# A Hyena encoder layer with a SwiGLU mixer: the way into the gate products, the last gate/up pair and the closing rows rewritten

## The chip, the cores and the metric

The kernel runs on one core of one Trainium2 chip. A core has TensorE (PE, which multiplies 128x128 weights into moving tiles of up to 512 columns and adds up in PSUM), VectorE (DVE), ScalarE (ACT), GpSimd (POOL) and SyncE (SP), each with its own in-order queue, and 16 DMA engines that the queues feed. The metric is the device time of one execution in microseconds; less is better.

## What is computed

One layer on a sequence of 1024 tokens with 1024 channels, in float32:

```
h = rmsnorm(x, norm_mix)
z = short_conv(h @ w_in + b_in);  x0, x1, v = split(z)          # 3 x 1024 channels
s = v * x1
y = irfft(rfft(s, 2L) * rfft(g, 2L))[:L] + s * skip              # g: filter made by a small MLP
x = x + (y * x0) @ w_out + b_out
x = x + (silu(n @ w_gate) * (n @ w_up)) @ w_down,  n = rmsnorm(x, norm_ffn)   # 2816 hidden
return rmsnorm(x, norm_final)
```

## The kernel before

Every product is done in three matmuls on split numbers: each operand is a high part rounded to the matmul's format ("fp32r") and a low part, the rest; high x high, high x low and low x high are added up in PSUM. `split(hi, lo, src)` casts the high part on ScalarE (L129) and subtracts on VectorE (L130). `low_dma(hi, lo, src)` makes the low part another way: ScalarE writes minus the high part (L149) and a DMA from GpSimd's queue adds the source to it (L150).

**Mixer, up to L1045.** The order of every engine is the order of the code (`manual_schedule`). At its end the last channel block goes through the inverse transform (`inverse`, `inverse_mm`, `finish`, `gate`) while TensorE multiplies the earlier blocks by `w_out`: `out_part(m, ks)` adds channel blocks `ks` of output columns 0 to 511 for the token blocks m and m + 4. Then `x1_half` adds such a half to the residual on VectorE, and ScalarE squares it and sums the squares into `sq2`.

**Into the gate products, L1236 to L1300.** TensorE, VectorE and ScalarE follow the code here, too. For the eight token blocks in the order `seq`, TensorE makes the other 512 columns (`out_mm`, 24 matmuls), `x1_half` adds them, `normed` scales by the reciprocal root of the mean square, `turn` transposes on TensorE, and `top_left` (blocks 0 to 3) or `top_sums` (blocks 4 to 7) make the moving operands of the gate and up products from the transposes. These products use a two-by-two block scheme with seven products instead of eight: of the normalised input they need the blocks B11, B21 (in `u2` for tokens 0 to 511), B22, T4 (in `u2` for tokens 512 to 1023) and the sums T1, T2, T3. Of each, `...h` is the high and `...l` the low part; in `u2` these are `uh` and `ul`.

**Gate/up pairs, `pair(i)`, i from 0 to 10.** A `Unit` is one of the two matrices for 256 hidden columns. It has products named by their weights' letter: a (`p1`, B11), f (T2), g (T3), e (T1), b (`p2`, B21), d (T4), c (B22), 12 matmuls each. a and b share a PSUM bank `pa`, f has `pb` (both in tile `...ab`); e and c share `pd`, g and d share `pc` (both in tile `...dc`). VectorE adds the banks into `uu` (L1203 after f, L1207 after g) and into the outputs (L1213 after e, L1217 after d and c). A product waits for VectorE when it writes a tile of which a bank is still to be read. The weights' operands rotate through five slots (`OPS`). For pair 0, part of them is made ahead (`pre`, `pq`, `wg0f` and so on). In the pairs only SP follows the code; TensorE, VectorE and ScalarE follow the order of a list scheduler that simulates the program when it is built. The gated products go to DRAM (`HD`) through GpSimd's queue, those of pair 10 through SP's (`held`).

**Down, from L1353.** Seven products `p1` to `p7` of 132 matmuls each add up in four PSUM banks (`bx`, `by`, `bz`); operands come from DRAM into raw slots `hr` (`HRAW`) and `wd`, which take over slots of the pairs (the tiles of T1, T2, T3 and `u2` among them) once those are read. The last product holds back three batches so that the four banks end one after another: for each, `scale(j)` adds, squares, takes the root on ScalarE, corrects the reciprocal by a Newton step, scales the two halves of a row block and stores them.

Of the kernel before, what the change touches and what calls it, by code (L numbers as in the profile page):

```python
# [102 lines left out]
def hyena_ffn_kernel(ctx: ExitStack, tc: tile.TileContext, a: dict, out: bass.AP):  # L103
# [377 lines left out]
    F_, Z_ = {}, {}  # L481

    class Filter:
# [534 lines left out]
    wo_split(1, 3)  # L1018

# [12 lines left out]
    def x1_half(j, h, o):  # L1032
        c = slice(h * 512, (h + 1) * 512)
        V.tensor_tensor(x1[j][:, c], x1[j][:, c], o, ALU.add)
        S.activation(
            slot("junk", f"jq{j}{h}", (512,)), x1[j][:, c], AF.Square, accum_out=sq2[j][:, h : h + 1]
        )
        load(X1D[j][:, c], x1[j][:, c])

    for m in range(4):  # L1040
        out_part(m, (NB - 1,))
        for q, j in enumerate(PAIRS[m]):
            x1_half(j, 0, po[m][:, q * 512 : (q + 1) * 512])
            V.tensor_scalar(sq2[j][:, 0:1], sq2[j][:, 0:1], 1.0 / D, EPS, ALU.mult, ALU.add)
# [12 lines left out]
    def normed(j):  # L1057
        w = small(f"rq{j}", 32, tag="rs1", bufs=2)
        sc, rt, r0, q = (w[:, i : i + 1] for i in range(4))
        V.scalar_tensor_tensor(sc, sq2[j][:, 1:2], 1.0 / D, sq2[j][:, 0:1], ALU.mult, ALU.add)  # L1060
        S.sqrt(rt, sc)
# [4 lines left out]
        for h in range(2):  # L1066
            d = x1[j][:, h * 512 : (h + 1) * 512]
            V.scalar_tensor_tensor(d, d, r0, gffn[:, h * 512 : (h + 1) * 512], ALU.mult, ALU.mult)

# [17 lines left out]
    def top_sums(m, pt):  # L1087
        ms = cols_of(m)
        if m < 3:
            tt = slot("inv", f"tt{m}", (4, 4, P))  # L1090
            t3, t2, t1, t4 = (tt[:, i] for i in range(4))
        else:
            ta, tb = slot("s1", "tta", (2, 4, P)), slot("xz", "ttb", (2, 4, P))
            t3, t2, t1, t4 = ta[:, 0], ta[:, 1], tb[:, 0], tb[:, 1]
        left = x1[m].rearrange("p (i k m) -> p i k m", i=2, k=4)
        b12, b22 = pt[:, 0:4], pt[:, 4:8]

        def part(nm, src, eng):
            hi, lo = tops[nm]
            S.copy(hi[:, :, ms], src)  # L1100
            n = 4 // len(lo)
            for x, l in enumerate(lo):
                ks = slice(x * n, (x + 1) * n)
                eng.tensor_tensor(l[:, :, ms], src[:, ks], hi[:, ks, ms].bitcast(F32), ALU.subtract)
# [3 lines left out]
        V.tensor_tensor(t2, b22, t1, ALU.subtract)
# [18 lines left out]
    OPS = ("fwd2", "vz", "s1", "xz", "sT")  # L1127
# [9 lines left out]
    class Unit:  # L1137
        def __init__(u, i, w, nm):
            u.nm = f"{nm}{i}"
# [24 lines left out]
        def sum_tiles(u):  # L1164
            u.s = slot(u.s_tag, f"{u.nm}s", (4, 4, P))

        def product(u, pt, x, src, bn, first, t=None):
            t = w_op(f"{u.nm}{x}", src) if t is None else t
            b = b_op(bn)
            for k in range(4):  # L1170
# [28 lines left out]

        def middle(u, early=False):  # L1200
            t = u.early if early else {}
            u.product(u.pb, "f", u.s[:, 1], "T2", True, t.get("f"))
            V.tensor_tensor(u.uu[:, 1], u.uu[:, 0], u.pb, ALU.add)  # L1203
# [3 lines left out]
            V.tensor_tensor(u.uu[:, 2], u.uu[:, 1], u.pc, ALU.add)  # L1207
            u.product(u.pd, "e", u.s[:, 0], "T1", True, t.get("e"))

        def end(u, out, early=False):  # L1210
            if not early:
                u.sum4()
            V.tensor_tensor(out[:, 2], u.uu[:, 2], u.pd, ALU.add)  # L1213
            u.product(u.pc, "d", u.a22, "T4", False)
            u.product(u.pd, "c", u.s[:, 3], "B22", False)
            u2b = u.uu[:, 1:2].broadcast_to([P, 2, 512])
            V.tensor_tensor(out[:, 0:2], u2b, u.dc.rearrange("p (q c) -> p q c", q=2), ALU.add)  # L1217
# [18 lines left out]
    with tc.manual_schedule(  # L1236
# [3 lines left out]
        for n, j in enumerate(seq):  # L1240
# [32 lines left out]
        ug.begin()  # L1273
        uu_.begin(True)
        ug.sums(V)
# [267 lines left out]
```

## Time and profile before

| what | value |
|---|---|
| median of 3 runs | 1182.83 us (1182.07 to 1184.84) |
| profiled execution, its own time | 1182.12 us |
| span of that execution, first to last instruction | 1180.3 us |
| mean granted TensorE clock | 0.995 |
| busy: PE, DVE, ACT, POOL | 1154.2, 875.5, 516.7, 151.2 us |

A row of a timeline has start, duration, engine, line, operation, output and inputs, and in brackets the idle time before it with what ended it. A row of waits has the engine that waited, what it was about to do, what it waited for, and the sum, the count and the longest in us. A row of the chain has start, duration, engine, tile and line. Matmuls overlap: the record of one lasts 0.39 us, and the next starts 0.23 us after it.

### The profile page before, as it was taken

What the parts mean: (1) busy time and instruction counts of PE and PEld (TensorE: products, weight loads), DVE (VectorE), ACT (ScalarE), POOL (GpSimd) and SP (SyncE); (2) the same over time, 40 slices, a digit from 0 to 9 for tenths busy, and PEclk for the clock granted to TensorE, in tenths of its full rate; (3) what the DMA queues carried; (4) which work ended last, traced back from release to release, by engine and by line L of the source; (5) the groups of instructions that cost most, each with busy time, mean ns of one, the idle gap of its engine ahead of it and who ended that gap; (6) DMA issues with size and microseconds to landing.
All of it is one profiled execution on the core that took longest, in us unless ns stands there. A gap on an engine that the chain in (4) does not pass through costs nothing.

```text
span 1180.3 us, 15139 instructions
## 1 busy us (share of the span) xinstructions
PE 1154.2 (98%) x5714; PEld 969.9 (82%) x5714; DVE 875.5 (74%) x1414; ACT 516.7 (44%) x820; POOL 151.2 (13%) x216
## 2 busy tenths in 40 slices
PE   8999999999999999898999999999999989999997
PEld 6889898898988987786888888888888868888885
DVE  7688988989898894588747676566666468956675
ACT  7563553545445473465333322332333233334444
POOL 0010211112011140043101110011001100111000
PEclk9999999999999999999999999999999999999999
DMA  7556778686675899443313232223323369842323
GB/s 236 147 120 144 141 164 166 159 174 149 131 154 109 206 242 271 135 117 72 118 61 125 99 133 89 91 97 126 107 72 113 111 193 365 302 121 89 98 81 143
DMA packets 100568, 170.32 MB, mean 144 GB/s; under 512 B 7052, under 2 KB 60684, under 8 KB 100367
## 3 DMA queue, kind: packets, MB, share of 16 engines
q0 software_dynamic: 24832, 78.39, 28.7%
q1 hardware_dynamic: 75661, 90.96, 23.6%
q8 instruction: 45, 0.74, 0.3%
q14 instruction: 28, 0.23, 0.1%
q10 hardware_dynamic: 2, 0.00, 0.0%
HBM read 101.96 MB, written 40.11 MB: 120 GB/s over the span
## 4 chain that ended last, share of the span: by engine, by line
PE 49%; DVE 4%; DMA 3%; issue 2%; ACT 1%; SPq 0%; POOL 0%; POOLq 0%; ACTq 0%; DVEq 0%
PE bx L1416 7%; PE po L914 3%; PE bz L1416 3%; PE by L1416 3%; DVE wd L1459 1%; PE wg0dc L1172 1%; PE wu9dc L1172 1%; PE wu8dc L1172 1%; PE wu7dc L1172 1%; PE wg9dc L1172 1%; PE wg8dc L1172 1%; PE wg7dc L1172 1%; PE wu6dc L1172 1%; PE wg6dc L1172 1%; PE wu5dc L1172 1%
## 5 line engine op out<-in xcount | busy, mean ns | idle before, releaser
L140 PE MATMUL z<-uh,whl 128*128 128x512 f32 x704 | 195.5, 393 | 0.0
L140 PEld LDWEIGHTS z<-uh,whl 128*128 128x128 f32 x704 | 130.1, 188 | 25.5
L1416 PE MATMUL bx<-wop,hop 128*128 128x512 f32 x480 | 111.1, 391 | 1.3 <-ACT hop L129 0.8
L140 PE MATMUL z<-ul,whl 128*128 128x512 f32 x352 | 108.8, 390 | 0.0
L1416 PEld LDWEIGHTS bx<-wop,hop 128*128 128x128 f32 x480 | 89.8, 188 | 21.4 <-ACT hop L129 1.2
L130 DVE TENSOR_TENSOR hop<-hrp,hop 128x1024 fp32r<-128x1024 f32 (+1 forms) x40 | 45.1, 1128 | 49.4 <-ACT hop L129 49.4
L129 ACT CAST hop<-hrp 128x1024 fp32r<-128x1024 f32 (+1 forms) x40 | 39.0, 977 | 91.9 <-PE bx L1416 44.6
L140 PEld LDWEIGHTS z<-ul,whl 128*128 128x128 f32 x352 | 66.1, 188 | 14.0
L914 PE MATMUL po<-wohl,uh 128*128 128x512 f32 x256 | 74.7, 394 | 1.8 <-DVE sig L669 1.4
L1027 POOL DMA_DIRECT2D hd<-g x40 | 21.6, 543 | 323.9 <-DVE g L1332 188.1
L1416 PE MATMUL by<-wop,hop 128*128 128x512 f32 x264 | 60.2, 389 | 0.0
L1416 PEld LDWEIGHTS by<-wop,hop 128*128 128x128 f32 x264 | 49.6, 188 | 10.3
L914 PEld LDWEIGHTS po<-wohl,uh 128*128 128x128 f32 x256 | 47.3, 188 | 12.4 <-DVE sig L669 1.6
L194 ACT CAST whl<-wt 128x1024 fp32r<-128x1024 f32 x24 | 25.2, 1049 | 68.7 <-PE z L140 64.7
L129 ACT CAST wop<-wd 128x512 fp32r<-128x512 f32 x73 | 42.2, 617 | 17.8 <-PE by L1416 9.2
L541 PE MATMUL pg<-hw,fwd 128*128 128x128 f32 x256 | 49.6, 275 | 0.0
L540 PE MATMUL pg<-hw,fwd 128*128 128x128 f32 x256 | 49.5, 275 | 0.0
L130 DVE TENSOR_TENSOR wop<-wd,wop 128x512 fp32r<-128x512 f32 x73 | 47.6, 684 | 1.5 <-ACT wop L129 1.5
L150 POOL DMA_DIRECT2D whl<-wt x24 | 20.8, 866 | 217.7 <-ACT whl L149 130.6
L1027 POOL DMA_DIRECT2D hrp<-hd x42 | 22.3, 531 | 187.0 <-DVE hop L130 166.9
L914 PE MATMUL po<-wohl,ul 128*128 128x512 f32 x128 | 44.3, 390 | 0.0
L540 PEld LDWEIGHTS pg<-hw,fwd 128*128 128x128 f32 x256 | 39.5, 192 | 0.6
(1586 smaller groups left out, 2834.9 us busy)
## 6 DMA issues: line engine op xcount, KB each, us to landing
hrp<-hd POOLq DMA_DIRECT2D x35, 512.0 KB, 4.0
wt<-in_hy_w_in_dram SPq DMA_DIRECT2D x24, 512.0 KB, 5.0
whl<-wt POOLq DMA_DIRECT2D x24, 512.0 KB, 4.6
wgr<-in_ffn_w_gate_dram SPq DMA_DIRECT2D x22, 512.0 KB, 4.1
wur<-in_ffn_w_up_dram SPq DMA_DIRECT2D x22, 512.0 KB, 3.9
wd<-in_ffn_w_down_dram SPq DMA_DIRECT2D x44, 256.0 KB, 6.6
hd<-g POOLq DMA_DIRECT2D x40, 256.0 KB, 2.6
hd<-sx POOLq DMA_DIRECT2D x30, 256.0 KB, 3.0
```

The costliest lines, as they stand in the source:

```text
L129: S.copy(hi, src)
L130: (eng or V).tensor_tensor(lo, src, hi.bitcast(F32), ALU.subtract)
L140: T.matmul(pt[:, h * 512 : (h + 1) * 512], w[wi], u2[ui][h][:, k, :], start=first and ti == 0, stop=last and ti == len(TERMS) - 1,)
L150: G.dma_start(lo.bitcast(F32), src, accum_op=ALU.add)
L194: S.copy(whl[:, 0], w_raw[n])
L540: T.matmul(o, fwd[r][:, j, :], f.hw[:, j, 0, :], start=True, stop=False)
L541: T.matmul(o, fwd[2 * r][:, jj, :], f.hw[:, jj, 1, :], start=False, stop=True)
L914: T.matmul(o, u2[yi][th][:, k, m * P : (m + 1) * P], wos[h][k // 2][wi][:, k % 2, :], start=(k == 0 and ti == 0), stop=(k == NB - 1 and ti ...
L1027: G.dma_start(dst, src)
L1172: T.matmul(pt, t[:, wi, k, :], b(k)[ui], start=first and k == 0 and ti == 0, stop=k == 3 and ti == len(TERMS) - 1, skip_group_check=not first,
L1416: T.matmul(pt, ho[hi_][:, x, q * P : (q + 1) * P], wo_[wi][:, x, :], start=fresh and first and x == 0 and ti == 0, stop=last and x == n - ...
L1459: V.tensor_tensor(w[:, dst], w[:, x], w[:, y], ALU.subtract)
```

## The change

1. `inverse_mm` of the last block stands between the parts of `out_part(.., (6,))` instead of behind all of them: eight matmuls come after it. `wo_load(1, 3)` uses another slot and is issued earlier. An instruction that loads ScalarE's square-root table stands behind the mixer's last split.
2. The squares are scaled by 1/32 while they are squared, so that their sums are means; the `sq2` correction (L1044) and its counterpart in `right` (L1474) go, and EPS is added where the two halves are.
3. `top_sums` becomes a class `Right` whose steps can be called one by one. The low parts of `top_left` for blocks 0 to 2, and for blocks 6 and 7 those of T4, for block 6 those of T3 and T1, are made by `low_dma`; of blocks 6 and 7 no low part is left on GpSimd's own arithmetic.
4. Blocks 6 and 7 and pair 0 are written out in a new order: block 6 is transposed before a of the gate unit, the steps of `Right` stand between the products, six matmuls of the up unit's b move behind g, and e, d and c of the gate unit follow each other, before f and g of the up unit. More weight operands of pair 0 are made ahead.
5. Pair 10 is `last_pair`: gate and up products interleaved, with TensorE in the order of the code. `HRAW` names other slots, and the last two slots of `OPS` change places.
6. The held-back batches of the last product follow the code on TensorE, VectorE and ScalarE, with the banks in the order 0, 2, 1, 3. `scale` takes the reciprocal of `sc / root + root`, with `gfin` doubled once, in place of the Newton step: three small VectorE operations behind the root instead of four. ScalarE scales and stores the right half first; the very last of these stores is issued from ScalarE's queue.

The core of the diff:

```diff
     wo_load(1, 2, "wt")
+    wo_load(1, 3, "hs")
     wo_split(1, 1)
     x1_load(5)
-    wo_load(1, 3, "whl1")
-    for m in range(3):
-        out_part(m, (6,))
+    out_part(0, (6,))
+    out_part(1, (6,), (0, 1))
     inverse_mm(b)
+    out_part(1, (6,), (2,))
+    out_part(2, (6,))
     finish(b)
...
     wo_split(1, 3)
+    S.sqrt(warm, ones)
...
         S.activation(
-            slot("junk", f"jq{j}{h}", (512,)), x1[j][:, c], AF.Square, accum_out=sq2[j][:, h : h + 1]
+            slot("junk", f"jq{j}{h}", (512,)),
+            x1[j][:, c],
+            AF.Square,
+            scale=1.0 / 32.0,
+            accum_out=sq2[j][:, h : h + 1],
         )
...
             x1_half(j, 0, po[m][:, q * 512 : (q + 1) * 512])
-            V.tensor_scalar(sq2[j][:, 0:1], sq2[j][:, 0:1], 1.0 / D, EPS, ALU.mult, ALU.add)
...
         S.copy(u2[0][0][:, :, ms], pt)
-        S.copy(x1[m].rearrange("p (k m) -> p k m", k=NB), pt)
+        xt = x1[m].rearrange("p (k m) -> p k m", k=NB)
+        S.copy(xt, pt)
+        if m < 3:
+            low_dma(u2[0][0][:, :, ms], u2[1][0][:, :, ms], xt)
+            return lambda: None
...
+        def low(t, nm, eng):
             hi, lo = tops[nm]
...
+                if eng is None:
+                    low_dma(hi[:, ks, t.ms], l[:, :, t.ms], t.src(nm)[:, ks])
+                else:
+                    eng.tensor_tensor(
+                        l[:, :, t.ms], t.src(nm)[:, ks], hi[:, ks, t.ms].bitcast(F32), ALU.subtract
+                    )
...
-    OPS = ("fwd2", "vz", "s1", "xz", "sT")
+    OPS = ("fwd2", "vz", "s1", "sT", "xz")
...
-        ug.begin()
+                ug.s_tag = "ab_d"
+                ug.split_sum_tiles()
+                ug.sums(V)
+        ug.begin(True)
         uu_.begin(True)
-        ug.sums(V)
-        low_dma(pq[:, 0, 0], pq[:, 0, 1], ug.a12)
-        normed(7)
+        r6 = Right(2, turns[6])
+        r6.sums12()
+        norm_begin(7)
+        r6.sum3()
+        r6.high("T2")
+        r6.b22_high()
+        norm_end(7)
+        ug.p1(pre[:, 0])
+        r6.high("T3")
+        r6.low("T3", None)
         early_op(pq[:, 1], uu_.a12)
-        ug.p1(pre[:, 0])
-        turn(6)
+        r6.low("T2", V)
+        r6.b22_low()
         ug.p1_out()
-        ug.early = {"f": w_op("wg0f", ug.s[:, 1])}
+        ug.early = {"f": w_op("wg0f", ug.s[1])}
         uu_.p1(pre[:, 1])
-        post(6)
-        post_late()
         turn(7)
+        r6.sum4()
+        r6.high("T1")
+        r6.low("T1", None)
         uu_.p1_out()
+        r7 = Right(3, turns[7])
+        r7.sums12()
+        r7.sum3()
         ug.p2(pq[:, 0])
-        post(7)
-        uu_.p2(pq[:, 1])
+        uu_.p2(pq[:, 1], (0, 1))
+        r6.t4_high()
+        r6.t4_low(None)
+        r7.part("T2", V)
+        r7.part("T3", V)
         ug.sum3()
...
+        ug.product(ug.pb, "f", None, "T2", True, ug.early["f"])
+        V.tensor_tensor(ug.uu[:, 1], ug.uu[:, 0], ug.pb, ALU.add)
+        r7.t4_high()
+        r7.t4_low(None)
+        r7.b22_high()
+        r7.b22_low()
+        ug.product(ug.pc, "g", None, "T3", True, ug.early["g"])
+        uu_.p2(pq[:, 1], (2, 3))
+        V.tensor_tensor(ug.uu[:, 2], ug.uu[:, 1], ug.pc, ALU.add)
+        ug.product(ug.pd, "e", None, "T1", True, ug.early["e"])
...
+        ug.end_products(g0[:, 1:4])
...
+    def last_pair(i):
...
+        ug.p1()
+        ug.p1_out()
+        ug.sums(V)
+        uu.p1()
+        uu.p1_out()
+        ug.product(ug.pb, "f", ug.s[1], "T2", True)
+        V.tensor_tensor(ug.uu[:, 1], ug.uu[:, 0], ug.pb, ALU.add)
+        ug.sum3()
+        ug.product(ug.pc, "g", ug.s[2], "T3", True)
+        V.tensor_tensor(ug.uu[:, 2], ug.uu[:, 1], ug.pc, ALU.add)
+        ug.p2()
+        S.activation(g[:, 0], ug.pa, AF.Silu)
+        ug.product(ug.pd, "e", ug.s[0], "T1", True)
+        uu.sums(V)
+        uu.product(uu.pb, "f", uu.s[1], "T2", True)
+        V.tensor_tensor(uu.uu[:, 1], uu.uu[:, 0], uu.pb, ALU.add)
+        ug.end(g[:, 1:4])
+        S.activation(g[:, 1:4], g[:, 1:4], AF.Silu)
+        uu.sum3()
+        uu.product(uu.pc, "g", uu.s[2], "T3", True)
+        V.tensor_tensor(uu.uu[:, 2], uu.uu[:, 1], uu.pc, ALU.add)
+        uu.p2()
+        V.tensor_tensor(g[:, 0], g[:, 0], uu.pa, ALU.mult)
+        uu.product(uu.pd, "e", uu.s[0], "T1", True)
...
-    HRAW = ("hs", "wt", "sT", "fwd2")
+    HRAW = ("hs", "wt", "fwd2", "s1")
...
+            for q in (0, 2, 1, 3) if held else range(4):
+                for x, ((ho, wo_), n) in enumerate(rest):
+                    mms(banks[q], ho, wo_, q, n, fresh, False, x == len(rest) - 1)
+                done(q)
...
-        V.scalar_tensor_tensor(sc, e, 1.0 / D, sqs[:, j : j + 1], ALU.mult, ALU.add)
+        V.scalar_tensor_tensor(sc, e, EPS, sqs[:, j : j + 1], ALU.add, ALU.add)
         S.sqrt(rt, sc)
-        V.reciprocal(r0, rt)
-        V.scalar_tensor_tensor(q, sc, -0.5, r0, ALU.mult, ALU.mult)
-        V.tensor_tensor(q, q, r0, ALU.mult)
-        V.scalar_tensor_tensor(r0, q, 1.5, r0, ALU.add, ALU.mult)
+        V.reciprocal(q, rt)
+        V.scalar_tensor_tensor(q, sc, q, rt, ALU.mult, ALU.add)
+        V.reciprocal(r0, q)
         a, b = y1[j][:, 0:512], y1[j][:, 512:1024]
+        S.activation(b, b, AF.Copy, scale=r0)
         V.scalar_tensor_tensor(a, a, r0, gfin[:, 0:512], ALU.mult, ALU.mult)
+        (S if j == NB - 1 else nc.sync).dma_start(ov[:, j, 512:1024], b)
         load(ov[:, j, 0:512], a)
-        S.activation(b, b, AF.Copy, scale=r0)
-        load(ov[:, j, 512:1024], b)
```

Where the code moves instructions, three pieces of the engines' order show it. The first is VectorE at the first residual halves (`x` a residual block, `po` the product's bank, `sq` the sums of squares, `rq` the small tile of `normed`). Before:

```order
L1034 TENSOR_TENSOR x_3689<-x_3689,po_3780 128x512
L1034 TENSOR_TENSOR x_3693<-x_3693,po_3910 128x512
L1044 TENSOR_SCALAR sq_3842<-sq_3842 128x1
L1034 TENSOR_TENSOR x_3776<-x_3776,po_3780 128x512
L1044 TENSOR_SCALAR sq_3842<-sq_3842 128x1
L1060 SCALAR_TENSOR_TENSOR rq_3939<-sq_3842 128x1
```

And of the change:

```order
L1037 TENSOR_TENSOR x_3672<-x_3672,po_3488 128x512
L1037 TENSOR_TENSOR x_3763<-x_3763,po_3488 128x512
L1037 TENSOR_TENSOR x_3674<-x_3674,po_3765 128x512
L1037 TENSOR_TENSOR x_3761<-x_3761,po_3765 128x512
L1037 TENSOR_TENSOR x_3678<-x_3678,po_3888 128x512
L1065 SCALAR_TENSOR_TENSOR rq_3917<-sq_3828 128x1
```

All eight adds now follow each other, and the add of the first other half (`po_3888`, before `po_3910`) stands behind them all, straight before the first small operation of its norm.

The second is ScalarE between block 6 and block 7 in pair 0 (`tt` and `tta`, `ttb` the sums of block 6 and of block 7, `wg0u` and `wu0u` the copies of a's banks, `wg0f` the operand of f). Before:

```order
L1185 COPY wg0u<-wg0ab 128x512
L129 CAST wg0f<-wg0s 128x512
L1106 COPY tt_4385<-tp_4360 128x512
L1100 CAST T2h<-tt_4385 128x4x128
L1100 CAST T3h<-tt_4385 128x4x128
L1100 CAST T1h<-tt_4385 128x4x128
L129 CAST uh_62<-tt_4385 128x4x128
L1116 CAST uh_62<-tp_4360 128x4x128
L1185 COPY wu0u<-wu0ab 128x512
L1106 COPY tta<-tp_4402 128x512
L1100 CAST T2h<-tta 128x4x128
```

And of the change:

```order
L149 ACTIVATE T3l_3957<-T3h 128x2x128
L153 CAST pq<-wur_4166 128x512
L149 ACTIVATE pq<-pq 128x512
L1250 COPY wg0u<-wg0ab 128x512
L129 CAST wg0f<-wg0sa 128x512
L1127 CAST T1h<-tt_4327 128x4x128
L149 ACTIVATE T1l<-T1h 128x4x128
L1250 COPY wu0u<-wu0ab 128x512
L1116 COPY tta<-tp_4381 128x512
L1149 CAST uh_62<-tt_4327 128x4x128
L149 ACTIVATE ul_64<-uh_62 128x4x128
L1127 CAST T2h<-tta 128x4x128
```

The copy `wg0u`, for which the gate unit's b waits, now stands behind block 6's T2, T3 and `pq`, and the negative copies for the lows (L149) stand between it and block 7's `T2h`.

The third is VectorE in pair 10 (`wg10..`, `wu10..` are the two units' operands and sums, `hop` and `wop` operands of the down stage, `g` the gated output). Before:

```order
L1213 TENSOR_TENSOR g_6995<-wg10u,wg10dc 128x512
L130 TENSOR_TENSOR wu10f<-wu10s,wu10f 128x512
L130 TENSOR_TENSOR wu10e<-wu10s,wu10e 128x512
L130 TENSOR_TENSOR hop12ct_g<-hrp_7329,hop12x_7331 128x1024
L1217 TENSOR_TENSOR g_6995<-wg10u,wg10dc 128x1024
L130 TENSOR_TENSOR wu10b<-wur_7122,wu10b 128x512
L1203 TENSOR_TENSOR wu10u<-wu10u,wu10ab 128x512
L1207 TENSOR_TENSOR wu10u<-wu10u,wu10dc 128x512
L130 TENSOR_TENSOR hop_7297<-hrp_7295,hop_7297 128x1024
```

And of the change:

```order
L1275 TENSOR_TENSOR g_6984<-wg10u,wg10dc 128x512
L130 TENSOR_TENSOR wu10b<-wur_6991,wu10b 128x512
L1477 TENSOR_TENSOR wu10u<-wu10u,wu10ab 128x512
L130 TENSOR_TENSOR wu10e<-wu10s,wu10e 128x512
L130 TENSOR_TENSOR wop_7290<-wd_7240,wop_7290 128x512
L130 TENSOR_TENSOR wop_7290<-wd_7241,wop_7290 128x512
L130 TENSOR_TENSOR wu10d<-wur_6991,wu10d 128x512
L1281 TENSOR_TENSOR g_6984<-wg10u,wg10dc 128x1024
L130 TENSOR_TENSOR wu10c<-wu10s,wu10c 128x512
L1482 TENSOR_TENSOR wu10u<-wu10u,wu10dc 128x512
L1484 TENSOR_TENSOR g_6984<-g_6984,wu10ab 128x512
L130 TENSOR_TENSOR hop_7287<-hrp_7285,hop_7287 128x1024
```

The add of the up unit's f (L1477, before L1203) now stands ahead of the wide sum of the gate unit's d and c and of every `hop`, and the first splits of the down weights (`wop`) stand ahead of the add after g (L1482).

More of the change, by code (lines that the diff above doesn't have):

```diff
@@ L1055, in t_op, with norm_begin, norm_end @@
         tops[nm] = (hi, lo)
[L1057 to L1061, printed above, removed]
+    def norm_begin(j):
+        w = rqs[j] = small(f"rq{j}", 32, tag="rs1", bufs=2)
+        V.scalar_tensor_tensor(w[:, 0:1], sq2[j][:, 1:2], EPS, sq2[j][:, 0:1], ALU.add, ALU.add)
+        S.sqrt(w[:, 1:2], w[:, 0:1])
+    def norm_end(j):
+        sc, rt, r0, q = (rqs[j][:, i : i + 1] for i in range(4))
         V.reciprocal(r0, rt)
@@ L1164, in sum_tiles, with split_sum_tiles, product @@
         def sum_tiles(u):
-            u.s = slot(u.s_tag, f"{u.nm}s", (4, 4, P))
-        def product(u, pt, x, src, bn, first, t=None):
+            t = slot(u.s_tag, f"{u.nm}s", (4, 4, P))
+            u.s = [t[:, q] for q in range(4)]
+        def split_sum_tiles(u):
+            ta, tb = slot("fwq", f"{u.nm}sa", (2, 4, P)), slot(u.s_tag, f"{u.nm}sb", (2, 4, P))
+            u.s = [ta[:, 0], ta[:, 1], tb[:, 0], tb[:, 1]]
+        def product(u, pt, x, src, bn, first, t=None, ks=range(4)):
             t = w_op(f"{u.nm}{x}", src) if t is None else t
             b = b_op(bn)
-            for k in range(4):
+            for k in ks:
                 for ti, (wi, ui) in enumerate(TERMS):
@@ L1212, in end @@
                 u.sum4()
[L1213 to L1217, printed above, removed]
+            u.end_products(out)
+            u.end_sums(out)
     seq = (0, 4, 1, 5, 2, 3, 6, 7)
@@ L1296, in hyena_ffn_kernel @@
+        ug.early["d"] = w_op("wg0d", ug.a22)
         uu_.sum_tiles()
         uu_.sums(V)
+        uu_.early["f"] = w_op("wu0f", uu_.s[1])
+        ug.end_products(g0[:, 1:4])
         uu_.sum3()
+        uu_.early["g"] = w_op("wu0g", uu_.s[2])
+        S.activation(g0[:, 0], ug.pa, AF.Silu)
+        ug.end_sums(g0[:, 1:4])
         uu_.sum4()
-        uu_.early = {}
+        uu_.product(uu_.pb, "f", None, "T2", True, uu_.early["f"])
+        V.tensor_tensor(uu_.uu[:, 1], uu_.uu[:, 0], uu_.pb, ALU.add)
@@ L1302, in hyena_ffn_kernel @@
+        uu_.product(uu_.pc, "g", None, "T3", True, uu_.early["g"])
     held = []
     def pair(i, ug=None, uu_=None):
-        put = store if i < NP - 1 else lambda *x: held.append(x)
-        g = slot("inv", f"g{i}", (4, 512))
         early = ug is not None
+        g = g0 if early else slot("inv", f"g{i}", (4, 512))
         if not early:
@@ L1431, in product2 @@
         rest = [(operands(nm, hx, wsrc, i, n), n) for i, n in BATCH[late:]]
-        for q in range(4):
-            for x, ((ho, wo_), n) in enumerate(rest):
-                mms(banks[q], ho, wo_, q, n, fresh, False, x == len(rest) - 1)
-            done(q)
+        with ExitStack() as order:
+            if held:
+                order.enter_context(
+                    tc.manual_schedule(
+                        engines={
+                            mybir.EngineType.PE,
+                            mybir.EngineType.DVE,
+                            mybir.EngineType.Activation,
+                        }
+                    )
+                )
+            for q in (0, 2, 1, 3) if held else range(4):
+                for x, ((ho, wo_), n) in enumerate(rest):
+                    mms(banks[q], ho, wo_, q, n, fresh, False, x == len(rest) - 1)
+                done(q)
     def four(fn, nm):
@@ L1502, in hyena_ffn_kernel @@
     load(gfin, a["norm_final"].partition_broadcast(P))
+    V.tensor_scalar(gfin, gfin, 2.0, None, ALU.mult)
     for i in range(NP):
```

160 lines of the change are left out of this document (106 added, 54 removed).

## The prediction

> **What bounds the kernel now.** I read the page's busy times first, then a table of engine times by stage, then TensorE's own waits.
>
> ```profile
> span 1180.3 us, 15139 instructions
> PE 1154.2 (98%) x5714; PEld 969.9 (82%) x5714; DVE 875.5 (74%) x1414; ACT 516.7 (44%) x820; POOL 151.2 (13%) x216
> ```
>
> TensorE is busy for 1154.2 of 1180.3 us and the change removes no matrix product, so at most 26 us can come back, plus whatever runs at a lowered clock. VectorE is not the bound: its work counts only where TensorE waits for it. The stages (columns after the stretch: length; then PE, PEld, DVE, ACT, POOL busy; granted clock; DMA share; GB/s):
>
> ```profile
> 448.00:490.00 42.00, 36.73 (x179) 29.92 (x178) 16.64 (x37) 15.46 (x29) 2.58 (x3) 1.00 0.76 231
> 528.00:556.00 28.00, 24.20 (x103) 18.32 (x102) 23.71 (x39) 16.33 (x30) 9.70 (x8) 0.94 0.37 72
> 556.00:944.00 388.00, 388.00 (x1714) 321.49 (x1713) 250.11 (x364) 119.08 (x183) 39.48 (x73) 1.00 0.31 103
> 944.00:955.00 11.00, 8.45 (x31) 6.51 (x30) 8.51 (x12) 4.61 (x7) 0.53 (x1) 0.84 0.39 121
> 980.00:1028.00 48.00, 47.89 (x212) 39.40 (x211) 44.17 (x67) 18.42 (x28) 3.76 (x8) 1.00 0.98 367
> 1164.00:1181.00 17.00, 7.67 (x33) 5.70 (x31) 8.27 (x28) 6.27 (x16) 0.00 (x0) 0.86 0.33 124
> ```
>
> The long middle, 556 to 944, has no idle TensorE at all. The idle time lies in four short places, and the change touches all four: the end of the mixer with the first residual halves (5.3 us idle), the first gate/up pair (3.8, with the clock at 0.94), the last pair (2.6, clock 0.84) and the closing rows. The waits name what is late there:
>
> ```profile
> PE tp L1073 <- DVE x L1068: 3.3, 1, 3.3
> PE wu10ab L1172 <- DVE wu10u L1203: 2.5, 1, 2.5
> PE wg0dc L1172 <- ACT wg0g L129: 1.9, 1, 1.9
> PE po L914 <- DVE sig L669: 1.4, 1, 1.4
> PE wu0ab L1172 <- ACT wu0u L1185: 1.0, 1, 1.0
> PE wg0dc L1172 <- DVE wg0u L1207: 0.9, 1, 0.9
> PE bx L1416 <- ACT hop L129: 0.8, 1, 0.8
> ```
>
> Below, times are on the clock of this trace, and "matmul" means 128x512, which repeats every 0.227 us at full clock (twelve take 2.72).
>
> **A, mixer end and first residual halves.** Eight matmuls (1.8 us) move from before the last inverse transform to behind it. They cover the 1.4 us that TensorE waited for `finish`, if the transform's input `vv` is ready 1.8 us earlier:
>
> ```profile
> 449.67 1.29 DVE L466 SCALAR_TENSOR_TENSOR vv<-y7ab 128x512 f32<-128x512 f32 x2
> 453.59 0.49 PE L653 MATMUL py<-inv,vv 128*128 128x128 f32 x2 [0.26 <-DVE rn L663]
> DVE sq L1044 <- ACT jq L1035: 7.6, 8, 2.3
> 483.13 0.68 DVE L1034 TENSOR_TENSOR x<-x,po 128x512 f32<-128x512 f32 x1
> 485.39 1.28 ACT L1061 ACT_TABLE_LOAD   x1
> 488.50 1.32 PE L1073 MATMUL tp<-ident,x 128*128 128x128 f32 x8 [3.29 <-DVE x L1068]
> ```
>
> `vv` ends at 450.96; the transform would start near 451.2, so it just fits: 1.4 gained. Next, the eight small `sq` operations go. Each kept VectorE waiting in order for ScalarE (7.6 us in eight waits), so the add that feeds the first normalised block came only at 483.1. TensorE ran dry at 485.2 (488.5 less 3.3); that add's own product ended 24 matmuls earlier, at 479.8. Without the `sq` operations the adds keep pace with the products (two adds of 0.7 to six matmuls of 1.4), and the table load of 1.3 moves ahead, under matmuls. From 479.8 the first block's chain is: add 0.7, square with its read-out 0.8, five small operations with the root near 1.2, two scalings 1.4: ready at 483.9, ahead of 485.2. The 3.3 us go whole. A = **4.7**; bounds 3.0 (`vv` late, the rest given) to 5.2 (the slow first transposes after the gap go too).
>
> **B, the first pair.** Here VectorE work goes to ScalarE (a negative copy) and a GpSimd-queue DMA that adds the original; three 1.2 us lows, one T3, one T1 and two T4 lows travel so. None removes a VectorE operation from the tightest spot; what counts is a new fixed order. The rows for its pieces:
>
> ```profile
> 535.44 0.62 ACT L1100 CAST T2h<-tt 128x512 fp32r<-128x512 f32 x1 [1.60 <-DVE tt L1108]
> 536.09 0.69 DVE L1104 TENSOR_TENSOR T2l<-tt,T2h 128x512 fp32r<-128x512 f32 x1
> 531.93 1.28 POOL L150 DMA_DIRECT2D pq<-wur  x1 [0.25 <-ACT pq L149]
> DMA to landing us min/median/max: 4.2/4.5/4.7
> 542.85 2.96 DVE L1104 TENSOR_TENSOR T3l<-tta,T3h 128x256 fp32r<-128x256 f32 x2
> 547.11 4.88 PE wg0dc L1172 x12
> ```
>
> A ScalarE or VectorE pass over 128x512 costs 0.6 in a row of them, a low by DMA 4.5 from issue to landing (four rows, `pre` and `pq`). Laying the changed order out with these, from 528.1, where the last output product ends: block 6 is transposed at once, both p1 products follow, and block 7's transpose runs at 534.5 as now (its norm sits behind 1.3 us of weight sums). Then ScalarE is the pacer: with its three negative copies and `pq` it reaches `T2h` of block 7 at 540.4, so VectorE's `T2l` ends at 541.1. TensorE has by then waited about 0.7 (for the copy `wg0u`) and 0.8 (for `pq`'s low, issued 535.5, landed 540.0). Product f runs 541.0 to 543.7, and g follows with no wait to 546.4; now it starts at 547.1. The reason is in the row at 542.85: two T3 lows that should cost near 0.4 each took 1.5 each beside GpSimd's own elementwise lows, and those are gone. Six held-back b matmuls cover part of the next add; e runs 548.2 to 550.9 after 0.4. Then d waits 1.8, since VectorE has `wu0f`'s low ahead of the add that frees the bank. d and c end at 558.1. In the trace g ends at 552.0, e starts after the 0.9 wait and ends at 555.7, and d, c (done later) cost 5.4, which makes 561.1 for the same work. B = **3.0**; bounds 0.8 (g at half pace once more, 4.88 instead of 2.72) and 6.7 (no wait beyond 539.4).
>
> The Trainium skill ("TensorE: Matmul & The Clock Gate", Part 1) lowers the clock only after an idle window of about 3.4 us. The trace differs: 1.9 us of waiting sufficed before the 4.88 us row. By the page no wait of mine would slow anything; by the row a third chance of 2.2 us stands, which I take as -0.5 after the sum.
>
> **C, the last pair.** The trace has b of `wu10` straight after the last f matmuls, so it waits 2.5 for the add of f, which stood behind two 1.2 us operations, and then runs at half pace:
>
> ```profile
> 943.62 1.23 DVE L130 TENSOR_TENSOR hop12ct_g<-hrp,hop12x 128x1024 fp32r<-128x1024 f32 x1 [2.45 <-ACT hop12x L129]
> 947.33 4.58 PE wu10ab L1172 x12
> 965.60 0.53 POOL L1027 DMA_DIRECT2D hrp<-hd  x1 [4.75 <-PE wu10dc L1172]
> hrp<-hd POOLq DMA_DIRECT2D x35, 512.0 KB, 4.0
> DMA to landing us min/median/max: 3.8/5.6/7.9
> ```
>
> In the new order d, c and g (8.2 us) stand between f and b, and b between g and e, each longer than the add it covers. That gives 2.5 and the half pace, 4.58 - 2.72 = 1.9. The third raw tile of the down stage no longer sits in a slot that the last up product holds (the 4.75 wait at 965.60), so the 0.8 wait for `hop` goes. Against it: g of `wu10` now comes late, and the first two raw tiles of the down stage take the T3 low's slots, free only after g. From there 5.4 us of matmuls remain, against 4.0 landing, 1.0 and 1.2 for the split: about 1.2 lost, the wait for the last VectorE add before e included. C = 2.5 + 1.9 + 0.8 - 1.2 = **4.0**; bounds 0.6 (landing at 7.9) and 5.2 (nothing lost).
>
> **D, the closing rows.** Four banks end one by one. Now the first two finish together, and the last row block goes like this:
>
> ```profile
> 1164.89 7.11 PE L1416 MATMUL bx<-wop,hop 128*128 128x512 f32 x30 [0.33 <-DVE y L1442]
> 1172.50 0.68 DVE L1442 TENSOR_TENSOR y<-y,bx 128x512 f32<-128x512 f32 x1
> 1173.57 0.63 ACT L1467 ACTIVATE jf<-y 128x512 f32<-128x512 f32 x1 [1.02 <-DVE rf L1486]
> 1174.20 0.71 ACT L1490 ACTIVATE y<-y,rf 128x512 f32<-128x512 f32 x1
> 1174.81 0.19 ACT L1482 ACTIVATE rf<-rf 128x1 f32<-128x1 f32 x1
> 1175.81 0.75 DVE L1488 SCALAR_TENSOR_TENSOR y<-y,rf,gfin 128x512 f32<-128x512 f32 x1
> 1174.06 3.33 SPq L126 DMA_DIRECT2D out_dram<-y  x4
> ```
>
> TensorE ends at 1172.0; the last scaling starts 3.8 later, held up by the previous block's scalings on both engines (0.5 before the add, 0.4 before the square, 0.3 before the root). In the fixed order that block is done. The same chain undisturbed, in the same units (0.7 add, 0.8 square, root and small operations 1.1, one of them fewer), is 2.6: 1.2 gained. The 0.3 wait goes, and one store on ScalarE's queue saves one 0.33 issue. D = **1.8**; bounds 0.8 and 2.3. The doubled `gfin` (one pass, about 1.2 us) falls where TensorE is fed by earlier splits; uncovered it would cost its 1.2.
>
> **Sum.** 4.7 + 3.0 + 4.0 + 1.8 = 13.5, less 0.5 for the clock: 13.0. The span becomes 1167.3. The profiled execution took 1182.12, 1.8 above its span, and would take 1169.1; the median is 0.7 above it, so **1169.8 us**.
>
> **Rivals.**
> 1. *Half the gain is stopped in the down stage.* Between 980 and 1028 DMA is at 0.98 of its share and 367 GB/s, and the chain of waits runs through its loads there. If loads were fixed in time, A to C would be spent waiting and only D stay: 1181.0. Against it: the queue of loads starts behind the last pair's stores and shifts with them, and VectorE finishes those sums about 3 us sooner after the last product. Chance 0.08 for this or for VectorE's removed work being merely cover (no change at all, 1182.8).
> 2. *The new lows arrive late.* Twelve rows of the same kind (`ul<-yr`, 256 KB) took 7.6 at the median, 3.1 more than 4.5:
>
> ```profile
> ul<-yr POOLq DMA_DIRECT2D x12, 256.0 KB, 7.6
> ```
>
> `pq` then delays f by 3.1, T4 delays d a little, and B is nothing: 1172.9, or 1176 with C at its low bound as well. For it: GpSimd's queue serves one issue of 1.28 after another. Against it: the four rows that landed in 4.2 to 4.7 stand in this same stage, where DMA share is 0.37. Chance 0.15. The skill's page "SBUF — State Buffer" (the "DVE blocks DMA" trap) would favour it: a VectorE pass in a two-port mode can hold up the descriptors of a GpSimd-queue DMA, 3.1 instead of 0.6 us in its example. The issue at 531.93 took its 1.28 with VectorE scaling block 7 beside it, which speaks against it.
> 3. *Slower: TensorE drops to half clock through the whole first pair.* The fixed order leaves a wait in nearly every stretch of 3 to 4 us from 535 to 553. If each keeps the clock down as in the 4.88 us row (0.18 us more a matmul), some 90 matmuls lose 16 us, more than the 13.5 gained: about 1186. It decides once more than 75 matmuls run so. Against it: in the trace the clock recovered after twelve. Chance 0.03.
>
> **How the numbers follow.** The forecast has 0.74. Its own bounds, the small terms not failing together, reach from 1166 (B without waits, C without loss) to 1173; rival 2 stretches this to 1176, and I stop there: **1166 to 1176**. A change under 0.2% (2.4 us) can't be told from none. Faster by more holds the forecast and rival 2 and part of rival 1's ground between: 0.91; same, the rest of rival 1: 0.06; slower: 0.03.
>
> **What would show it.** A: no TensorE wait for `x` before the first transpose, none for `sig`, and the square-root table load before 470. B: f starting 3 to 4 us after block 7's transposes plus p2, T3 lows of 0.4 each, g at 2.7, and a wait of 1 to 2 before d. C: no wait of `wu10ab` for the add of f, a wait of about 1 at the first `bx` for `hop`. D: less than 3 us from the last matmul to the last scaling. Wrong would be: matmuls at half pace between 530 and 560, new idle time of TensorE between 970 and 1030, or a span above 1172.

## The result, and the profile after

The changed kernel takes **1176.04 us** (median of 5 runs, 1174.12 to 1177.2) against 1182.19 for the kernel before beside it: ratio **0.9939** (95% interval 0.9928 to 0.995), so 6 to 8.5 us or 0.6% faster. (The ratio is estimated from the runs of both kernels; the quotient of these two medians is 0.9948, or 6.2 us. Gains below go by the ratio, and 0.9939 is 7.2 us.) The prediction was 1169.8 with a range of 1166 to 1176: the sign was right, the time came out at the very edge of the range, and the gain to a little over half of the 13.0 us forecast.

The profiled execution is the slowest of the five, so its span is 4.9 us below that of before, a little less than the medians say. Its first lines:

```profile
span 1175.4 us, 15154 instructions
PE 1151.6 (98%) x5714; PEld 970.0 (83%) x5714; DVE 870.8 (74%) x1389; ACT 522.3 (44%) x829; POOL 155.1 (13%) x218
```

VectorE lost 4.7 us of work, ScalarE and GpSimd's queue gained. Where the time went is read from the table of engine times by stage of the changed kernel (length; PE, PEld, DVE, ACT, POOL busy with the count of instructions; granted clock; DMA share; GB/s):

```profile
448.00:490.00 42.00, 41.02 (x203) 34.23 (x202) 17.64 (x36) 19.15 (x35) 4.01 (x4) 1.00 0.76 238
490.00:528.00 38.00, 34.95 (x170) 28.67 (x167) 26.10 (x54) 21.93 (x41) 15.43 (x14) 0.96 0.74 138
528.00:556.00 28.00, 22.26 (x91) 17.20 (x90) 20.29 (x38) 15.82 (x31) 8.23 (x7) 0.94 0.76 115
930.00:980.00 50.00, 50.00 (x223) 41.40 (x222) 29.97 (x39) 18.84 (x26) 6.47 (x13) 1.00 0.66 229
```

TensorE's count is a ruler: the kernels do the same products, and one matmul is 0.227 us. By 490 the changed kernel is 24 or 25 ahead of before (203 against 179 in this stage, and one more ahead of it): 5.7 us gained, part A. Then it falls back: 170 against 185 in the residual loop, 91 against 103 in pair 0. At 556 it stands 2 *behind*. DMA share rose from 0.44 to 0.74 in the loop and from 0.37 to 0.76 in pair 0, for only 28 and 43 GB/s more. Part B was to gain 3.0 and lost 27 matmuls, 6.1 us. The last pair has no idle TensorE left (50.00 of 50). The loop before, for comparison:

```profile
490.00:528.00 38.00, 37.73 (x185) 30.76 (x184) 30.84 (x63) 21.87 (x43) 11.49 (x10) 1.00 0.44 110
```

TensorE's waits between 440 and 575 in the changed kernel:

```profile
PE wu0ab L1237 <- DMA pq<-wur: 2.6, 1, 2.6
PE tp L1085 <- issue: 2.2, 1, 2.2
PE wg0dc L1237 <- DVE g L1275: 1.3, 1, 1.3
PE wg0ab L1237 <- DMA pre<-wgr: 1.2, 1, 1.2
PE tp L1085 <- DVE x L1076: 0.9, 1, 0.9
PE wg0ab L1237 <- ACT wg0u L1250: 0.8, 1, 0.8
```

The waits for `sig` and for `x` before the first transposes are gone, as forecast. The waits for `pq` (0.8 forecast) and `pre` (none forecast) are for transfers. The waits at `tp` are transfers too, at one remove, as the chain of waits of this stretch shows (start, duration, what ran or was waited for):

```profile
490.65 6.06 DMA xd<-x
496.74 0.75 DVE x L1076
...
515.52 4.18 DMA xd<-x
519.72 0.75 DVE x L1076
520.48 0.64 DVE x L1037
521.13 4.54 DMA xd<-x
...
537.15 5.29 DMA pq<-wur
542.48 1.20 PE wu0ab L1237 x4
543.68 4.33 PE wg0ab L1237 x12
548.01 2.75 PE wg0dc L1237 x12
```

`xd<-x` is the store of a finished residual half to DRAM (`X1D`). The next step scales that half in place, so VectorE has to wait until the store has read it. Three times the chain runs through this store, for 4.2 to 6.1 us.

At the end, the last scaling of the changed kernel starts 2.6 us after the last matmul (1167.8), before 3.8:

```profile
1170.44 0.72 ACT L1645 ACTIVATE y<-y,rf 128x512 f32<-128x512 f32 x1 [0.68 <-DVE rf L1643]
1170.44 0.75 DVE L1646 SCALAR_TENSOR_TENSOR y<-y,rf,gfin 128x512 f32<-128x512 f32 x1
```

### The profile page after: what moved, and what is told of

Same layout as the page of the kernel before. It is cut to its first block, busy times and chain, and to the rows that moved or that the text cites. A ratio compares the mean times of both kernels' runs of the same rounds, so it can differ in the third digit from the quotient of the medians.

```text
span 1175.4 us, 15154 instructions
## 1 busy us (share of the span) xinstructions
PE 1151.6 (98%) x5714; PEld 970.0 (83%) x5714; DVE 870.8 (74%) x1389; ACT 522.3 (44%) x829; POOL 155.1 (13%) x218
## 4 chain that ended last, share of the span: by engine, by line
PE 85%; DVE 7%; DMA 6%; ACT 1%; issue 1%; POOL 0%; DVEq 0%; POOLq 0%; ACTq 0%; SPq 0%
PE z L140 20%; PE bx L1560 8%; PE po L914 3%; PE bz L1560 3%; PE by L1560 3%; PE pg L541 2%; PE pp L614 2%; PE pg L540 2%; DMA wd<-in_ffn_w_down_dram 2%; DMA xd<-x 1%; DMA wohl<-wo 1%; PE py L653 1%; PE py L654 1%; PE z L366 1%; PE z L693 1%; PE wu9dc L1237 1%
```

## Experiments: which part gains and which loses

The theory to test: A, C and D do what the trace shows, and B gives half of it back because the new low parts by DMA crowd out other transfers. The rival: the new order of pair 0 itself costs.

**A alone**, in the kernel before:

```diff
+    wo_load(1, 3, "hs")
     wo_split(1, 1)
     x1_load(5)
-    wo_load(1, 3, "whl1")
-    for m in range(3):
-        out_part(m, (6,))
+    out_part(0, (6,))
+    out_part(1, (6,), (0, 1))
     inverse_mm(b)
+    out_part(1, (6,), (2,))
+    out_part(2, (6,))
...
+    S.sqrt(warm, ones)
...
-            V.tensor_scalar(sq2[j][:, 0:1], sq2[j][:, 0:1], 1.0 / D, EPS, ALU.mult, ALU.add)
```

> The kernel before with part A alone (the eight moved matmuls, the scaled squares without the sq corrections, the table load ahead). Theory: A is a real gain of about 4.9 us that the other parts later give back, so about 1177.3 against 1182.2. Rival (the residual loop is held by its stores and loads, whatever comes earlier): the 4.9 us is spent in the loop and pair 0 even without the new lows, and the time stays within 1.5 us of the kernel before.

Measured: 1175.25, ratio 0.9945 (0.9932 to 0.9958). A alone (6.5 us) gains about as much as the whole change, and the loop and pair 0 take nothing of it back: 188 matmuls in the loop and 102 in pair 0, against 185 and 103 before.

**C alone**, in the kernel before:

```diff
-    OPS = ("fwd2", "vz", "s1", "xz", "sT")
+    OPS = ("fwd2", "vz", "s1", "sT", "xz")
...
-    for i in range(NP):
+    for i in range(NP - 1):
         pair(i, *((ug, uu_) if i == 0 else ()))
+    with tc.manual_schedule(engines={mybir.EngineType.PE}):
+        last_pair(NP - 1)
...
-    HRAW = ("hs", "wt", "sT", "fwd2")
+    HRAW = ("hs", "wt", "fwd2", "s1")
```

> The kernel before with part C alone (last_pair, HRAW and OPS swapped). Theory: about 3.3 us faster (the trace of the change shows 963.37 for the end of the last up product with four more bx matmuls done before it), about 1178.9. Rival (the down stage's loads take the gain back): within 1 us of the kernel before.

Measured: 1179.54, ratio 0.9974 (0.9965 to 0.9984), 3.1 us.

**D alone**, in the kernel before (with the rewritten `scale` and `right`, and `gfin` doubled):

```diff
-        for q in range(4):
+        with ExitStack() as order:
+            if held:
+                order.enter_context(tc.manual_schedule(engines={...}))
+            for q in (0, 2, 1, 3) if held else range(4):
```

> The kernel before with part D alone (closing order, scale in three small operations behind the root, gfin doubled). Theory: the tail behind the last matmul shrinks by 0.7 and the waits before it by 0.6, about 1.3 us faster, 1180.9. Rival (the banks' order changes nothing, since only the last bank's chain counts): 0.7 or less.

Measured: 1182.59, ratio 0.9999 (0.9989 to 1.0008): no difference that the runs can tell. In its profiled execution the stretch from the last 104 matmuls of the third down product to the end of the span is 150.9 us long (1027.35 to 1178.2) against 152.5 before (1027.81 to 1180.3), which is the forecast's size; but one execution does not settle what eleven leave open.

**A, C and D without B**, and **A and C alone**: the edits above together.

> The kernel before with A, C and D, without B (lows of the first blocks on VectorE and GpSimd, blocks 6, 7 and pair 0 in the old order). Theory: the three gains add up to about 9.5 us, 1172.7, so that B as a whole loses about 3.3 us of it in the kernel after (1176.0). Rival (B is neutral and the three don't add up): about 1176.

> The kernel before with A and C, without B and D. Theory (D is worth its shorter tail of 1.0 and its 0.3 wait when A and C stand, and D alone was hidden by scatter): about 1.3 slower than A, C and D together, 1171.4. Rival (D is worth nothing): 1170.

Measured: 1170.06, ratio 0.9896 (0.9883 to 0.9909), and 1171.35, ratio 0.9902 (0.9884 to 0.9919). Without B the kernel gains 12.3 us, 5.1 more than with it, and the intervals are far apart: **B as a whole costs 5 us**. The parts alone add up to 9.7 (6.5, 3.1, 0.1); the 2.6 more together are within what the intervals allow. D's worth is again in the right direction and within the scatter. The stages of A, C and D together, next to those of the changed kernel above:

```profile
448.00:490.00 42.00, 41.28 (x205) 34.51 (x204) 17.91 (x37) 18.32 (x34) 2.58 (x3) 1.00 0.76 238
490.00:528.00 38.00, 37.77 (x188) 30.86 (x186) 32.59 (x67) 23.30 (x47) 14.07 (x12) 1.00 0.49 116
528.00:556.00 28.00, 24.61 (x100) 18.36 (x99) 25.75 (x40) 14.13 (x24) 7.78 (x7) 0.94 0.30 70
```

The same start (205), then 188 matmuls in the loop where the changed kernel does 170, and 100 in pair 0 where it does 91.

## Experiments: what in B costs

**The lows of `top_left` back on VectorE**, the rest of the change kept:

```diff
         S.copy(xt, pt)
-        if m < 3:
-            low_dma(u2[0][0][:, :, ms], u2[1][0][:, :, ms], xt)
-            return lambda: None
         return lambda: V.tensor_tensor(
```

> The changed kernel with the low parts of top_left for blocks 0 to 2 back on VectorE, so that three accumulating DMAs of 512 KB fewer run in the residual loop. Theory (these DMAs slow the residual stores for which the in-place scaling waits, 5.3, 4.2 and 4.5 us in the chain): the store waits fall to about 2.6, and some 2 to 3 us come back, about 1173.5. Rival (the loss is in the new order of pair 0): within 0.5 us of the changed kernel, 1176.

Measured: 1171.25, ratio 0.9898 (0.9885 to 0.9911). Three DMAs fewer, 1.2 us more VectorE work for each, and **4.9 us** come back, more than I expected. (The first of the three waits that the expectation quotes is 6.1 in the chain above; 5.3 is what VectorE stood idle in all three together.) The loop is whole again and pair 0 nearly so:

```profile
490.00:528.00 38.00, 37.75 (x189) 30.88 (x188) 32.30 (x63) 21.58 (x44) 12.79 (x11) 1.00 0.50 118
528.00:556.00 28.00, 23.44 (x103) 17.96 (x102) 22.94 (x41) 17.70 (x32) 7.59 (x6) 1.00 0.61 104
```

What the three DMAs did is in the view of the DMA queues between 486 and 545 (`q0` is GpSimd's queue, `q1` SyncE's: packets, MB, share of 16 engines; then issues with count, size, median us to landing). The changed kernel:

```profile
q0 software_dynamic: 6574, 3.28, 49.9%
q1 hardware_dynamic: 2976, 3.67, 21.5%
...
ul<-x POOLq DMA_DIRECT2D x3, 512.0 KB, 7.9
...
pre<-wgr POOLq DMA_DIRECT2D x1, 256.0 KB, 8.5
```

And with those lows on VectorE:

```profile
q0 software_dynamic: 3712, 1.84, 28.0%
...
pre<-wgr POOLq DMA_DIRECT2D x1, 256.0 KB, 4.3
```

With the DMAs, GpSimd's queue has 2862 packets of about 500 bytes more and holds the 16 engines for 21.9% of 59 us more, 13 us. (The three lows are a little more than this: one 256 KB low of block 7 falls into this stretch only with the lows on VectorE. The next two versions give the three alone.) Bytes don't tell it: GpSimd's packets of 500 bytes took 72 ns each, SyncE's of 1.2 KB 68 ns, so that 3.28 MB held the engines more than twice as long as 3.67. What GpSimd's queue issues meanwhile lands later: the operand `pre` in 8.5 us instead of 4.3. The first residual store in the loop makes VectorE wait 3.4 us, and the next add comes 2.8 us later than without them. VectorE's timeline of the changed kernel:

```profile
496.74 0.75 DVE L1076 SCALAR_TENSOR_TENSOR x<-x,rq,gffn 128x512 f32<-128x512 f32 x1 [3.37 <-DMA xd<-x]
500.71 0.68 DVE L1037 TENSOR_TENSOR x<-x,po 128x512 f32<-128x512 f32 x1
```

And with the lows on VectorE, both scalings at once and no wait:

```profile
493.27 1.41 DVE L1076 SCALAR_TENSOR_TENSOR x<-x,rq,gffn 128x512 f32<-128x512 f32 x2
497.91 0.68 DVE L1037 TENSOR_TENSOR x<-x,po 128x512 f32<-128x512 f32 x1
```

**The lows of blocks 6 and 7 on VectorE**, those of `top_left` still by DMA; and **none of the new lows by DMA** (this edit and the one above):

```diff
-        r6.low("T3", None)
+        r6.low("T3", V)
...
-        r6.low("T1", None)
+        r6.low("T1", V)
...
-        r6.t4_low(None)
+        r6.t4_low(V)
...
-        r7.t4_low(None)
+        r7.t4_low(V)
```

> The changed kernel with the T3, T1 and T4 lows of blocks 6 and 7 on VectorE and the new order kept. Theory: pq and the weights' lows land earlier, but VectorE gets some 2.5 us more work in the first pair; about even, 1175 to 1177. Rival (these DMAs' landing is what the first pair waits for): 2 to 3 us faster, about 1173.5.

> The changed kernel with none of the new lows by DMA, the new order of pair 0 kept. Theory (the DMAs are what costs): 3 us or more faster than the changed kernel, 1173 or less. Rival (the order of pair 0 itself costs): about 1176 still.

Measured: 1176.49, ratio 0.9937 (0.9925 to 0.995), and 1169.37, ratio 0.9882 (0.9869 to 0.9894). The lows of blocks 6 and 7 alone change nothing: the loop still loses. Once the loop is whole they do count: without them 1.9 us more come back, and the runs of the two versions lie apart (1168.95 to 1169.66 against 1171.02 to 1171.48). Without any new low the kernel is 6.7 us faster than the change, so **the rival falls**: the order of pair 0, kept here, costs nothing against A, C and D with the old order (0.9896); whether it gains 1.7 us is within the intervals. With no new lows:

```profile
490.00:528.00 38.00, 37.74 (x188) 30.84 (x187) 32.57 (x66) 22.16 (x45) 12.79 (x11) 1.00 0.50 118
528.00:556.00 28.00, 24.04 (x104) 18.08 (x103) 25.30 (x44) 14.90 (x27) 1.28 (x1) 1.00 0.27 66
```

Four more matmuls by 556 than with the old order, 0.9 us; but the execution with the old order had the clock at 0.94 in pair 0, so this too settles nothing between the orders.

These two versions differ in the three lows alone. GpSimd's queue between 486 and 545, with and without them:

```profile
q0 software_dynamic: 5232, 2.62, 39.8%
```

```profile
q0 software_dynamic: 2112, 1.05, 15.7%
```

That is 1.57 MB in 24.1% of 59 us, 14.2 us, or 4.7 us of all 16 engines for each low.

**The stores without their consequence**: does the loop lose by the wait for the store?

```diff
-        load(X1D[j][:, c], x1[j][:, c])
+        load(X1D[j][:, c], gffn[:, c])
```

> The changed kernel with the residual stores reading the norm's weight tile instead of the residual: the same bytes at the same time, but no scaling waits for a store any more (left out: the stored residual is not the right one, so the final sum is not). Theory: the waits of the scalings in the loop go and about 3 us come back, 1173. Rival (the waits for the weights' lows and the order of pair 0 decide): 1 us or less.

Measured: 1176.9, ratio 0.9946 (0.9934 to 0.9958). The number looks like the rival's, but the stages say otherwise. This edit did more than it was meant to: with no residual to wait for, the stores went out early, in the mixer's last stage, and there the lows of `w_out` came late:

```profile
PE po L914 <- DMA wohl<-wo: 4.7, 3, 2.3
```

```profile
448.00:490.00 42.00, 37.03 (x181) 30.35 (x180) 15.86 (x30) 15.88 (x31) 2.58 (x3) 1.00 0.86 277
490.00:528.00 38.00, 38.00 (x191) 31.25 (x189) 28.18 (x61) 24.91 (x47) 16.32 (x14) 1.00 0.58 99
```

22 matmuls fewer in the stage up to 490, and then no idle time in the loop at all (38.00 of 38, 191 against 170), with the same three lows by DMA. So the lows cost the loop through the stores, and not by their own landing, nor by the three negative copies on ScalarE and the issues on GpSimd that come with them, which all stay here. This run took both the wait for the stores and their bytes out of the loop; that it is the wait is read from the chain and from VectorE's 3.4 us above, not shown by this run alone. The time of the whole kernel says nothing about it. The waits for lows in pair 0 stay (`pq` 2.5 us, `pre` 1.3).

**The same bytes in longer pieces**:

```diff
-            low_dma(u2[0][0][:, :, ms], u2[1][0][:, :, ms], xt)
+            S.activation(u2[1][0][:, :, ms], u2[0][0][:, :, ms].bitcast(F32), AF.Copy, scale=-1.0)
+            G.dma_start(u2[1][0][:, 2 * m : 2 * m + 2, :].bitcast(F32), x1[m].rearrange("p (k m) -> p k m", k=2), accum_op=ALU.add)
```

> The changed kernel with the same three accumulating DMAs of 512 KB in the residual loop, but each writing one contiguous stretch of 4 KB per partition in place of eight pieces of 512 bytes (left out: the low parts of blocks 0 to 2 land in the wrong columns, so the result is not the layer's). Theory (the small pieces occupy the DMA engines, which delays the stores and the weights' lows): the landing of pre returns toward 4.3 us, the scaling's wait for the store goes, and the time is near 1171 to 1172. Rival (it is the bytes and the accumulation, whatever the pieces): still about 1176.

Measured: 1194.49, ratio 1.0096 (1.0077 to 1.0114). Neither theory's number: a failed experiment as to the time. The stretches that the DMA now wrote still held operands of the output products of later blocks, and these waited for it. What it does show is the transfer itself, in the same stretch:

```profile
q0 software_dynamic: 1170, 1.94, 20.2%
...
ul<-x POOLq DMA_DIRECT2D x3, 512.0 KB, 4.6
```

```profile
PE po L914 <- DMA ul<-x: 17.1, 2, 8.9
```

4.6 us to landing for the 512 KB instead of 7.9, and 191 us of engine time, added up over the 16, for 1.94 MB instead of 471 for 3.28: 98 a megabyte instead of 144. The waits also spread the transfers out, so the shape's share in this isn't settled. The Trainium skill ("DMA: Bandwidth & Descriptors", Specifications) puts the least size for line rate at 512 bytes. For these accumulating transfers the two runs do not bear that out: with all pieces of just that size a megabyte took 144 us of engine time, with the three lows in longer ones 98.

## Experiments: can it be better

Two versions more. In the first, with none of the new lows by DMA, the gate unit's last output add stands ahead of the up unit's sums and operand f:

```diff
+        ug.end_products(g0[:, 1:4])
         uu_.sum_tiles()
         uu_.sums(V)
         uu_.early["f"] = w_op("wu0f", uu_.s[1])
-        ug.end_products(g0[:, 1:4])
```

> The changed kernel with none of the new lows by DMA, and the gate unit's last output add put ahead of the up unit's sums and f operand. Theory (the wait of 1.6 before d is that order): about 0.9 faster than without the new lows alone, 1168.5. Rival (VectorE's total work bounds the first pair): 1169.4, unchanged.

The second has this edit on the version with only `top_left`'s lows on VectorE, and `pq`'s low ahead of the T3 lows on GpSimd's queue:

```diff
+        early_op(pq[:, 1], uu_.a12)
         r6.high("T3")
         r6.low("T3", None)
-        early_op(pq[:, 1], uu_.a12)
```

> The changed kernel with top_left's lows on VectorE, the gate unit's last output add put ahead of the up unit's sums and f operand, and pq's low issued ahead of the T3 lows on GpSimd's queue. Theory (first pair: TensorE waits 1.7 for that add and 1.6 for pq, both orders of queues): some 2 us faster than with the lows on VectorE alone, 1169 to 1170. Rival (VectorE's total work is what bounds the first pair): 1171.

Measured: 1168.77, ratio **0.9876** (0.9856 to 0.9896), and 1170.32, ratio 0.989 (0.9872 to 0.9909). The wait that the edit aims at halves; with no new lows, before and after it:

```profile
PE wg0dc L1234 <- DVE g L1272: 1.6, 1, 1.6
```

```profile
PE wg0dc L1234 <- DVE g L1272: 0.9, 1, 0.9
```

In the second version the wait of 1.6 for `pq`, whose low stood behind the T3 lows in GpSimd's queue, is gone as well. The time follows by an amount within the intervals (0.9882 to 0.9876, 0.9898 to 0.989). The first of the two is the fastest kernel measured, some 14.7 us below before and 7.5 below the change.

## Why the prediction was right, and why it was 6 us short

| term | forecast | traces, before to after | kernels |
|---|---|---|---|
| A, mixer end | 4.7 | 5.0 at the first transposes, 5.7 by 490 | 6.5 (5.0 to 8.0) alone |
| B, first pair | 3.0 | -6.1, by matmuls done between 490 and 556 | -5.1 (the change against A, C and D alone) |
| C, last pair | 4.0 | 4.0 (the last 104 matmuls of `p3` start at 1024.24 instead of 1027.81, from 0.5 behind at 556) | 3.1 (1.9 to 4.1) alone |
| D, closing rows | 1.8 | 1.3 | 0.1 (-0.9 to 1.3) alone |

**A** held in every step: no wait for `sig`, none for `x` at the first transposes (483.5 instead of 488.5), the table load at 464.8. It is a little larger than its upper bound of 5.2.

**B is the step that failed**, at its price for "a low by DMA 4.5 from issue to landing (four rows, `pre` and `pq`)". Those rows were 256 KB transfers in stretches with a DMA share of 0.37 to 0.44. I used the figure for the lows that feed a product soon and gave the "three 1.2 us lows" of `top_left`, of 512 KB each, no price at all, since nothing waits for them before pair 0. But they hold the engines, 4.7 us each, and things do wait for what stands behind them: the scalings for the residual stores, which I did not look at, and then `pre` and `pq`. `pq`'s low was issued at 537.15 and landed at 542.44, not 535.5 and 540.0: its issue stood behind those of the two T3 lows (2.4 us from 535.7).

The rest of B's layout held: `wg0u` 0.8 (0.7 forecast), g without a wait and at 2.75 (2.7), two T3 lows in 0.75 together (0.4 each), a wait before d of 1.3 (1.8). Only f began at 543.5 instead of 541.0 and ran at half pace, which cost 1.6 us where the sum had 0.5 for the clock. The order was sound. Its lateness came in part from the loop, in part from its own lows: with the loop whole, TensorE still waits 1.6 us for `pq`, and 0.5 with no new low by DMA.

**Rival 2** ("the new lows arrive late") is the one that came nearest: the low of `pq` stood behind other issues and held f up by 2.6 us (3.1 in the rival), though it landed in 5.3 us and not in 7.6. Its time of 1172.9 to 1176 ends at the result. But it looked at `pq` and T4 and not at the three lows in the loop, and so stopped at B being nothing, where B is a loss. The rule of the Trainium skill that the prediction set beside it ("SBUF — State Buffer", on VectorE holding up descriptors) is neither borne out nor refuted by any run here.

**C and D** held in the traces in mechanism and size: no wait of `wu10ab`, 0.8 at the first `bx` for `hop`, 2.6 from the last matmul to the last scaling. D's 1.3 to 1.6 us of the traces was never shown in medians. **Rival 1** (the down stage takes the gain) is refuted: A, C and D together gained 12.3. **Rival 3** (half clock throughout) did not occur.

That the total still came out at the edge of the range is luck in this respect: B, at -5.1, lies far outside its own bounds of 0.8 to 6.7. The range reached up to 1176 because rival 2 set B to nothing and C to its low bound of 0.6 (by C's own terms nearer 0.1 to 0.5, which would have ended a little above 1176); instead B lost and C came nearly whole, and A, C and D together brought 12.3 us where the sum had 10.5. Two of the prediction's own signs of being wrong did show: f at half pace at 543.7, and a span of 1175.4 where it allowed 1172.

## What to carry to other kernels

A transfer that nothing waits for isn't free: price it by the time that its packets hold the DMA engines (here 72 ns for 500 bytes and 68 ns for 1.2 KB), not by its bytes, and list every transfer that lands in that time and who waits for it, stores that guard an in-place update included. A landing time read in a quiet stretch doesn't hold once three more transfers are put into it. Moving 1.2 us of VectorE work to DMA paid nothing where VectorE was not what TensorE waited for.

## What was not expected of the hardware

The length of a wait doesn't settle what TensorE's clock does after it. The same wait of 1.9 us before g of pair 0 was followed by half pace in four kernels (before, C alone, A with C, and A, C and D) and by full pace in two (A alone, D alone). Of the four, all but before waited another 0.2 to 0.4 us some matmuls later, which may have had its part. The wait of 3.3 us before the first transposes left the clock alone in two executions and halved it in D alone, at unchanged code:

```profile
488.99 1.78 PE L1073 MATMUL tp<-ident,x 128*128 128x128 f32 x8 [3.27 <-DVE x L1068]
490.42 1.20 PE L914 MATMUL po<-wohl,uh 128*128 128x512 f32 x2
...
491.85 1.05 PE L914 MATMUL po<-wohl,uh 128*128 128x512 f32 x2
```

And a wait of 2.57 us for `pq` in the changed kernel was followed by f in 4.33, while the kernel with the other stores ran on at full pace after this:

```profile
542.31 0.73 PE L1237 MATMUL wu0ab<-uh,pq 128*128 128x512 f32 x2 [2.55 <-DMA pq<-wur]
...
543.11 0.40 PE L1237 MATMUL wu0ab<-uh,pq 128*128 128x512 f32 x1
543.34 0.39 PE L1237 MATMUL wg0ab<-T2h,wg0f 128*128 128x512 f32 x1
```

The Trainium skill ("TensorE: Matmul & The Clock Gate", Part 1) says that the window of about 3.4 us runs freely, so that the point of change depends on where in it the work falls. That agrees with equal waits and unequal ends. That a whole idle window is needed does not agree: 1.9 us sufficed in before, and 2.1 to 2.3 in two pieces in three more. About 2 us in a single execution can hang on this (twelve matmuls in 4.33 to 4.88 instead of 2.72), which is nearly a third of the gain measured here.
